# An encoder block in one launch: the low halves of 56 stationary factors on VectorE instead of in an adding DMA, and w_down's plain chunk at the other end

## The chip, the cores and the metric

The kernel runs on one core of one Trainium2 chip. The metric is the device time of one execution in microseconds, the median of several runs.

## The reference

One layer of a streaming encoder on 512 positions with 2048 channels, all float32. A mixer (a projection, two causal depthwise convolutions, a gate, a layer norm, an output projection) comes first and is not touched. Behind it stands the MLP, which is what the change is about:

```python
m = rms_norm(h, mlp_pre_gain[l])
z = jnp.square(jax.nn.relu(jnp.einsum("bsd,df->bsf", m, w_up[l])))      # 2048 -> 8192
z = jnp.einsum("bsf,fd->bsd", z, w_down[l])                             # 8192 -> 2048
h = h + rms_norm(z, mlp_post_gain[l])
```

## The kernel before, in words

**Float32 products from two halves.** TensorE multiplies rounded values (type fp32r). Every factor is therefore kept as a high half, which is the value rounded by a copy on ACT, and a low half, which is the value less its high half. A product is three matmuls: high by low, low by high, high by high.

**Seven products instead of eight.** Most of the work goes by Strassen's scheme with seven products for a 2 x 2 arrangement of blocks. `by_seven` (L367) does a pair of output tiles of w_up with seven calls of `product` (L360), 24 matmuls each, in the order r11, t2, t1, r21, t3, r22, t4. `wide_seven` (L945) does the same for w_down, on one chunk of z and two blocks of 512 output columns, in seven groups of 24 matmuls. Sums of blocks of the weights and of the activations are made on VectorE beforehand. The first eight tiles of w_up, and one of the eight chunks of w_down's product, are plain: no seven products and no sums.

**Where stationary factors come from.** `Stationary` (L109) is one long list of jobs, one for each 128 x 1024 factor of w_in, w_out, w_up and w_down in the order of use. A raw weight block is loaded by SyncE (`load`, L119) into one of six raw buffers. A job's value is a raw block or a sum of blocks (VectorE, L163 for w_up, L195 for w_down). `prepare` (L228) makes the high half on ACT (L237) two jobs ahead of the low half, and the low half on VectorE (L246). `take` (L252) asks for the factors of the next product and prepares three or four more. In w_up's pairs the seventh job, and in w_down's units the eleventh and twelfth (`22a`, `22b`), are raw blocks, and for these 28 + 28 jobs the low half is made in another way: ACT writes minus the high half (L240), and a DMA that adds, issued by GpSimd (POOL in the profile), brings the raw block from HBM a second time and adds it to that (L241).

**Buffers.** One pool of 43 slots of 128 x 1024 holds all halves, sums, z tiles and moving factors. During w_up about thirty of them hold the moving side for the whole stage; the rest turn over. A slot is written again when its last reader is done, which for a z tile's half is the DMA that stores it.

**z.** w_up's output tile pairs, each a z tile of 128 x 2 x 512, go through `keep_z` (L783): relu, square and the high half on ACT (L790, L791, L796), the low half on VectorE (L340, the line of the helper `add`), and both halves stored to z_dram by DMAs that ACT issues (L811). Chunk c is made of z tiles 4c to 4c + 3. A chunk that is used in seven products also needs the sums of its blocks: two more VectorE steps, a high and a low half, two more stores. These steps are a queue of small jobs, `z_jobs`: three jobs a tile without sums, six with them. Each product of w_up runs one job, or two when more than eight are queued (L891), and each group of `wide_seven` runs one.

**w_down.** Chunks 0 to 6 go through `wide_seven`, four blocks of 512 columns in two calls each, and are added up in SBUF; while a chunk's second call runs, the next chunk's factors are loaded from z_dram (`load_factor`, L896, on SyncE's queue between the weights). Chunk 7 is plain and comes last: half of it in `wide_tile` (L1004), the other half in the loop that ends the kernel, row block by row block, with the norm and the output behind each. PSUM has seven banks for products; in both seven-schemes a bank is reused by a later product that adds onto it, so VectorE's evacuation (L340) must have read it by then.

**Order.** Nothing is scheduled by a tool: each engine's instructions stand in the order in which this code issues them. Evacuations are put off by one product (`pending`, L341).

## Time and profile before

| | |
|---|---|
| median of 3 runs | 2028.47 us (2028.08 to 2035.81) |
| the profiled execution | 2024.5 us, span 2022.8 us |
| mean granted TensorE clock | 0.987 of full speed |
| TensorE busy | 1919.6 us (95%) |
| VectorE busy | 1563.1 us (77%) |
| ScalarE (ACT) busy | 914.3 us (45%) |
| GpSimd (POOL) busy | 129.6 us (6%) |
| DMA moved | 372.17 MB, mean 184 GB/s |

The mixer takes the first 640 us or so. The MLP's norm and its plain tiles follow, the products of seven of w_up run from about 722 to 1358 us, w_down's from 1358 to about 1915, and its plain chunk ends the kernel. In a row of the timeline the first number is the start, the second how long, and in brackets stands how long the engine was idle before it and what ended that. In a row of waits stand the sum, how often, and the longest.

### The profile page before, as it was taken

The page shows a single profiled execution, that of the slowest core. Times are in us where ns is not written, and L with a number is a line of the kernel's source. Part 1 is how long each engine was busy: PE and PEld are TensorE (multiplying, and loading weights), DVE is VectorE, ACT ScalarE, POOL GpSimd, SP SyncE. Part 2 cuts the span into 40 slices and gives each one's busy share as a digit, 9 for nine tenths or more (in the row PEclk, how much of TensorE's full clock was granted, in tenths as well). Part 3 has the DMA queues.
Part 4 walks back from the last instruction along what each step waited for, and adds up shares of the span by engine and source line. Part 5 has one row for each costly group of instructions (what it writes and reads, how often), then busy time and mean ns, then how long its engine had stood idle before and what let it go on. Part 6 is the DMA issues. An engine that isn't in the chain of part 4 may idle for free.

```text
span 2022.8 us, 28179 instructions
## 1 busy us (share of the span) xinstructions
PE 1919.6 (95%) x11050; PEld 1696.6 (84%) x11050; DVE 1563.1 (77%) x1932; ACT 914.3 (45%) x1114; POOL 129.6 (6%) x126
## 2 busy tenths in 40 slices
PE   8999999999999977899999999898999999999998
PEld 6888888888998867899999999887887877877876
DVE  8899898669767767777877877758678787787748
ACT  6222121444445455555565565546534343353343
POOL 4000011201110000000000000000000000000000
PEclk9999999999999988999999999999999999999999
DMA  7233323233367357777777777677875866768732
GB/s 250 87 104 104 104 84 104 83 117 92 111 201 257 98 167 229 219 218 218 211 211 227 214 214 226 200 251 227 269 229 167 280 199 219 260 189 256 266 110 84
DMA packets 154357, 372.17 MB, mean 184 GB/s; under 512 B 12144, under 2 KB 75760, under 8 KB 154224
## 3 DMA queue, kind: packets, MB, share of 16 engines
q1 hardware_dynamic: 78192, 270.04, 40.6%
q10 hardware_dynamic: 67968, 70.96, 10.2%
q0 software_dynamic: 8064, 29.36, 7.6%
q8 instruction: 87, 1.43, 0.3%
q14 instruction: 46, 0.38, 0.1%
HBM read 295.35 MB, written 74.97 MB: 183 GB/s over the span
## 4 chain that ended last, share of the span: by engine, by line
PE 29%; DMA 16%; DVE 8%; issue 6%; ACT 4%; SPq 0%; ACTq 0%; DVEq 0%; POOLq 0%
PE bank L935 24%; DMA z_dram<-slot 7%; DMA slot<-w_up_in 6%; PE bank L299 4%; DVE slot L246 2%; DMA raw<-w_down_in 2%; DVE slot L340 2%; ACT slot L237 2%; DVE slot L163 1%; DVE slot L195 1%; DMA raw<-w_up_in 1%; ACT slot L791 1%; ACT slot L790 1%; ACT slot L796 0%; DVE raw L163 0%
## 5 line engine op out<-in xcount | busy, mean ns | idle before, releaser
L299 PE MATMUL bank<-slot,slot 128*128 128x256 f32 (+1 forms) x7584 | 1143.9, 313 | 64.5 <-DMA slot<-w_up_in 33.6
L299 PEld LDWEIGHTS bank<-slot,slot 128*128 128x128 f32 x7584 | 1057.5, 192 | 150.3 <-DMA slot<-w_up_in 38.5
L935 PE MATMUL bank<-slot,slot 128*128 128x512 f32 x2736 | 631.3, 392 | 19.3 <-DVE slot L340 11.6
L935 PEld LDWEIGHTS bank<-slot,slot 128*128 128x128 f32 x2736 | 514.8, 189 | 132.2 <-DVE slot L340 13.7
L237 ACT ACTIVATE slot<-raw 128x1024 fp32r<-128x1024 f32 x336 | 345.7, 1050 | 244.7 <-DVE raw L163 108.0
L237 ACT ACTIVATE slot<-slot 128x1024 fp32r<-128x1024 f32 x208 | 218.9, 1057 | 382.9 <-DVE slot L195 211.1
L246 DVE TENSOR_TENSOR slot<-raw,slot 128x1024 fp32r<-128x1024 f32 x280 | 349.8, 1263 | 46.1 <-ACT slot L237 40.5
L246 DVE TENSOR_TENSOR slot<-slot,slot 128x1024 fp32r<-128x1024 f32 x208 | 254.1, 1222 | 60.4 <-PE bank L299 23.3
L340 DVE TENSOR_TENSOR slot<-slot,slot 128x1024 fp32r<-128x1024 f32 (+2 forms) x128 | 104.7, 824 | 102.2 <-DMA z_dram<-slot 47.9
L510 DVE SCALAR_TENSOR_TENSOR slot<-slot,par_sb,slot 128x512 f32<-128x512 f32 x240 | 162.9, 743 | 0.0
L340 DVE TENSOR_TENSOR slot<-slot,bank 128x512 f32<-128x512 f32 x208 | 133.9, 680 | 27.8 <-PE bank L935 27.8
L195 DVE TENSOR_TENSOR slot<-slot,raw 128x1024 f32<-128x1024 f32 x28 | 34.3, 1225 | 78.2 <-DMA raw<-w_down_in 77.7
L94 ACT ACTIVATE slot<-tmp 128x512 fp32r<-128x512 f32 (+1 forms) x40 | 21.9, 583 | 155.4 <-DVE tmp L543 117.5
L319 PE MATMUL bank<-slot,slot 128*128 128x512 f32 (+1 forms) x216 | 80.6, 373 | 6.2 <-ACT slot L94 6.2
L321 PE MATMUL bank<-slot,slot 128*128 128x512 f32 (+1 forms) x216 | 80.5, 373 | 2.9 <-DVE slot L98 2.9
L320 PE MATMUL bank<-slot,slot 128*128 128x512 f32 (+1 forms) x216 | 80.3, 372 | 1.5 <-DVE slot L246 1.5
L241 POOL DMA_DIRECT2D slot<-w_up_in x28 | 24.5, 875 | 717.2 <-DVE slot L340 399.5
L796 ACT ACTIVATE slot<-slot 128x1024 fp32r<-128x1024 f32 x60 | 63.4, 1056 | 12.7 <-DVE slot L340 9.7
L417 POOL TENSOR_TENSOR sum<-sum,tmp 128x512 f32<-128x512 f32 x35 | 59.4, 1698 | 94.5 <-ACT tmp L421 93.3
L240 ACT ACTIVATE slot<-slot 128x1024 fp32r<-128x1024 f32 x56 | 59.4, 1060 | 1.8
L241 POOL DMA_DIRECT2D slot<-w_down_in x28 | 24.4, 870 | 527.8 <-ACT slot L240 375.5
L319 PEld LDWEIGHTS bank<-slot,slot 128*128 128x128 f32 x216 | 41.4, 192 | 13.1 <-ACT slot L94 6.2
(101 smaller groups left out, 982.5 us busy)
## 6 DMA issues: line engine op xcount, KB each, us to landing
raw<-w_up_in SPq DMA_DIRECT2D x128, 512.0 KB, 4.5
z_dram<-slot ACTq DMA_DIRECT2D x120, 512.0 KB, 5.9
slot<-z_dram SPq DMA_DIRECT2D x106, 512.0 KB, 8.2
raw<-w_down_in SPq DMA_DIRECT2D x100, 512.0 KB, 4.5
raw<-w_in_in SPq DMA_DIRECT2D x76, 512.0 KB, 4.4
raw<-w_out_in SPq DMA_DIRECT2D x32, 512.0 KB, 4.1
slot<-w_up_in POOLq DMA_DIRECT2D x28, 512.0 KB, 8.6
slot<-w_down_in SPq DMA_DIRECT2D x28, 512.0 KB, 5.9
```

The costliest lines, as they stand in the source:

```text
L237: nc.scalar.activation(hi, value, AF.Copy)
L240: nc.scalar.activation(lo, hi.bitcast(F32), AF.Copy, scale=-1.0)
L246: nc.vector.tensor_tensor(lo, value, hi.bitcast(F32), op=ALU.subtract)
L299: nc.tensor.matmul(ps, s, m, start=n == 0 and not onto, stop=n == len(todo) - 1, skip_group_check=onto)
L319: nc.tensor.matmul(ps[:, cols], hi, mhi, start=first, stop=False)
L320: nc.tensor.matmul(ps[:, cols], lo, mhi, start=False, stop=False)
L321: nc.tensor.matmul(ps[:, cols], hi, mlo, start=False, stop=last)
L340: add = lambda out, a, b, op=ALU.add: nc.vector.tensor_tensor(out, a, b, op=op)
L417: nc.gpsimd.tensor_tensor(self.total, self.total, t, op=ALU.add)
L510: nc.vector.scalar_tensor_tensor(out=acc, in0=g[:, k : k + S], scalar=w, in1=acc, op0=ALU.mult, op1=ALU.add)
L796: nc.scalar.activation(made["hi", g].rearrange("p f w -> p (f w)"), value.rearrange("p a b -> p (a b)"), AF.Copy,)
L935: matmul = lambda a, b, first=False, last=False: nc.tensor.matmul(ps, a, b, start=first, stop=last, skip_group_check=onto)
```

## The change

It has two parts.

First, the adding DMA goes. Every job of `Stationary` has its low half made on VectorE (L246 before, L239 after). With it go 56 copies on ACT (L240), 56 DMAs on POOL's queue (L241) and the second reading of those blocks. The low half's slot is taken when VectorE's instruction is issued and no longer with the high half, and the raw block of such a job is read last by VectorE and no longer by ACT.

Second, the plain chunk is chunk 0 instead of chunk 7. `wide_seven` runs over chunks 1 to 7, and chunk 0 still comes last. The z tiles without sums are thus the first four, not the last four, and the last four have them. The host lays w_down out accordingly. The queue of z jobs is drained by two from more than six on.

```diff
-            self.jobs.append((lambda: self.get(n), n + 1, None))
+            self.jobs.append((lambda: self.get(n), n + 1))
...
-                (lambda: self.get(n22), 4, odd[1] if added_up else None),
+                (lambda: self.get(n22), 4),
...
-                (lambda: raw("22a"), 5, units["22a"]),
-                (lambda: raw("22b"), 6, units["22b"]),
+                (lambda: raw("22a"), 5),
+                (lambda: raw("22b"), 6),
...
-                    hi, lo = slot([P, WCOLS], F32R), None
+                    hi = slot([P, WCOLS], F32R)
                     nc.scalar.activation(hi, value, AF.Copy)
-                    if added is not None:
-                        lo = slot([P, WCOLS], F32R)
-                        nc.scalar.activation(lo, hi.bitcast(F32), AF.Copy, scale=-1.0)
-                        nc.gpsimd.dma_start(lo, added, accum_op=ALU.add)
-                    self.high.append((value, hi, lo))
-                value, hi, lo = self.high[len(self.parts)]
-                if lo is None:
-                    lo = slot([P, WCOLS], F32R)
-                    nc.vector.tensor_tensor(lo, value, hi.bitcast(F32), op=ALU.subtract)
+                    self.high.append((value, hi))
+                value, hi = self.high[len(self.parts)]
+                lo = slot([P, WCOLS], F32R)
+                nc.vector.tensor_tensor(lo, value, hi.bitcast(F32), op=ALU.subtract)
...
-        if c == N_CHUNK - 1:
+        if c == 0:
             z_jobs.append([lambda: store(0, 1)])
             return
...
-        z_job(2 if len(z_jobs) > 8 else 1)
+        z_job(2 if len(z_jobs) > 6 else 1)
...
-    for c in range(N_CHUNK - 1):
-        following = WIDE_ORDER if c < N_CHUNK - 2 else FACTORS[:4]
+    for c in range(1, N_CHUNK):
+        following = WIDE_ORDER if c + 1 < N_CHUNK else FACTORS[:4]
+        c_next = (c + 1) % N_CHUNK
...
-        wide_tile(t, N_CHUNK - 1, range(CHUNK // 2), last_step)
+        wide_tile(t, 0, range(CHUNK // 2), last_step)
...
-                    ps, plain_block(N_CHUNK - 1, k, b), b % 2, parts[t, i // 2], i % 2,
+                    ps, plain_block(0, k, b), b % 2, parts[t, i // 2], i % 2,
```

TensorE's and SyncE's instructions stand in the same order before and after; only VectorE's, ACT's and POOL's lists differ. Line numbers shift by seven: L340 before is L333 after, L246 is L239, L195 and L163 stay.

VectorE in a regular pair of w_up, from the low half of a z tile (`slot<-slot,slot`) on, through an evacuation (`tmp<-tmp,bank`) and the sums of that z tile (128x512 and twice 128x256) to the next pair's sums of weights. Before:

```order
L340 TENSOR_TENSOR slot_7737<-slot_7409,slot_7701 128x1024
L340 TENSOR_TENSOR tmp_7657<-tmp_7656,bank_7739 128x256
L340 TENSOR_TENSOR slot_7772<-slot_7409 128x512
L340 TENSOR_TENSOR slot_7772<-slot_7409,slot_7772 128x256 x2
L163 TENSOR_TENSOR slot_7800<-raw_7694,raw_7696 128x1024
L163 TENSOR_TENSOR slot_7801<-slot_7800,raw_7523 128x1024
```

And after:

```order
L333 TENSOR_TENSOR slot_6711<-slot_6387,slot_6678 128x1024
L239 TENSOR_TENSOR slot_6740<-raw_6429,slot_6705 128x1024
L333 TENSOR_TENSOR tmp_6634<-tmp_6633,bank_6713 128x256
L333 TENSOR_TENSOR slot_6748<-slot_6387 128x512
L333 TENSOR_TENSOR slot_6748<-slot_6387,slot_6748 128x256 x2
L163 TENSOR_TENSOR slot_6776<-raw_6671,raw_6673 128x1024
L163 TENSOR_TENSOR slot_6777<-slot_6776,raw_6500 128x1024
```

One instruction is new, the second: the low half of the pair's seventh factor.

VectorE in the first pair of seven, from the evacuation of the third product (`tmp<-tmp,bank`) to that of the fifth (`slot<-tmp,bank`); L95 is the low half of an activation sum. Before:

```order
L340 TENSOR_TENSOR tmp_5866<-tmp_5865,bank_5977 128x256
L95 TENSOR_TENSOR slot_5436<-slot_5756,slot_5436 128x256
L95 TENSOR_TENSOR slot_5486<-slot_5756,slot_5486 128x256
L340 TENSOR_TENSOR slot_6018<-slot_5531,slot_6015 128x1024
L163 TENSOR_TENSOR slot_6044<-raw_5920,raw_5922 128x1024
L163 TENSOR_TENSOR slot_6045<-slot_6044,raw_5701 128x1024
L246 TENSOR_TENSOR slot_6050<-raw_5701,slot_6002 128x1024
L340 TENSOR_TENSOR slot_6054<-slot_5531 128x512
L340 TENSOR_TENSOR slot_6054<-slot_5531,slot_6054 128x256 x2
L246 TENSOR_TENSOR slot_6087<-slot_6045,slot_6048 128x1024
L340 TENSOR_TENSOR slot_5863<-tmp_5866,bank_6060 128x256
```

And after:

```order
L333 TENSOR_TENSOR tmp_5866<-tmp_5865,bank_5972 128x256
L95 TENSOR_TENSOR slot_5436<-slot_5756,slot_5436 128x256
L95 TENSOR_TENSOR slot_5486<-slot_5756,slot_5486 128x256
L163 TENSOR_TENSOR slot_6038<-raw_5920,raw_5922 128x1024
L163 TENSOR_TENSOR slot_6039<-slot_6038,raw_5701 128x1024
L239 TENSOR_TENSOR slot_6044<-raw_5701,slot_5997 128x1024
L333 TENSOR_TENSOR slot_6048<-slot_5703,slot_6012 128x1024
L239 TENSOR_TENSOR slot_6077<-slot_6039,slot_6042 128x1024
L333 TENSOR_TENSOR slot_5863<-tmp_5866,bank_6050 128x256
```

The sums are gone, and the low half of a z tile (L333, 128x1024) that stands here is of the tile after the one before. Just ahead of this place one more pair of sums is gone and one low half of a factor is new.

VectorE in a unit of w_down, the evacuations of two groups (`slot<-slot,bank`), two instructions each. Before:

```order
L340 TENSOR_TENSOR slot_13094<-slot_13094,bank_13725 128x512
L340 TENSOR_TENSOR slot_13094<-slot_13094,bank_13726 128x512
L340 TENSOR_TENSOR slot_13097<-slot_13097,bank_13769 128x512
L340 TENSOR_TENSOR slot_13097<-slot_13097,bank_13770 128x512
L246 TENSOR_TENSOR slot_13842<-slot_13598,slot_13806 128x1024
```

And after:

```order
L333 TENSOR_TENSOR slot_13064<-slot_13064,bank_13691 128x512
L333 TENSOR_TENSOR slot_13064<-slot_13064,bank_13692 128x512
L239 TENSOR_TENSOR slot_13764<-raw_13415,slot_13726 128x1024
L239 TENSOR_TENSOR slot_13770<-raw_13488,slot_13762 128x1024
L333 TENSOR_TENSOR slot_13067<-slot_13067,bank_13732 128x512
L333 TENSOR_TENSOR slot_13067<-slot_13067,bank_13733 128x512
L239 TENSOR_TENSOR slot_13806<-slot_13564,slot_13768 128x1024
```

The low halves of `22a` and `22b` now stand between the two groups' evacuations.

More of the change, by code (lines that the diff above doesn't have):

```diff
@@ L172, in p7 @@
                 return sub(self.get(n11), self.get(n11), self.get(n21))
-            for value, frees, added in (
-                (lambda: self.get(n11), 0, None),
-                (p6, 0, None),
-                (lambda: s["1"], 0, None),
-                (lambda: self.get(n12), 0, None),
-                (p7, 2, None),
-                (lambda: sub(s["2"], self.get(n12), s["2"]), 0, None),
-                (lambda: self.get(n22), 4, odd[1] if added_up else None),
+            for value, frees in (
+                (lambda: self.get(n11), 0),
+                (p6, 0),
+                (lambda: s["1"], 0),
+                (lambda: self.get(n12), 0),
+                (p7, 2),
+                (lambda: sub(s["2"], self.get(n12), s["2"]), 0),
+                (lambda: self.get(n22), 4),
             ):
-                self.jobs.append((value, n11 + frees if frees else 0, added))
+                self.jobs.append((value, n11 + frees if frees else 0))
         def strassen_wide(self, units):
@@ L208, in s2 @@
                 return sub(s[u], s[u], raw("11" + u))
-            for value, frees, added in (
-                (lambda: s1("a"), 0, None),
-                (lambda: s1("b"), 0, None),
-                (lambda: s2("a"), 0, None),
-                (lambda: s2("b"), 0, None),
-                (lambda: raw("11a"), 0, None),
-                (lambda: raw("11b"), 0, None),
-                (lambda: sub(raw("11a"), raw("11a"), raw("21a")), 2, None),
-                (lambda: sub(raw("11b"), raw("11b"), raw("21b")), 4, None),
-                (lambda: sub(s["a"], last["a"], s["a"]), 0, None),
-                (lambda: sub(s["b"], last["b"], s["b"]), 0, None),
-                (lambda: raw("22a"), 5, units["22a"]),
-                (lambda: raw("22b"), 6, units["22b"]),
-                (lambda: last["a"], 0, None),
-                (lambda: last["b"], 0, None),
+            for value, frees in (
+                (lambda: s1("a"), 0),
+                (lambda: s1("b"), 0),
+                (lambda: s2("a"), 0),
+                (lambda: s2("b"), 0),
+                (lambda: raw("11a"), 0),
+                (lambda: raw("11b"), 0),
+                (lambda: sub(raw("11a"), raw("11a"), raw("21a")), 2),
+                (lambda: sub(raw("11b"), raw("11b"), raw("21b")), 4),
+                (lambda: sub(s["a"], last["a"], s["a"]), 0),
+                (lambda: sub(s["b"], last["b"], s["b"]), 0),
+                (lambda: raw("22a"), 5),
+                (lambda: raw("22b"), 6),
+                (lambda: last["a"], 0),
+                (lambda: last["b"], 0),
             ):
-                self.jobs.append((value, first + frees if frees else 0, added))
+                self.jobs.append((value, first + frees if frees else 0))
         def prepare(self, upto):
@@ L279, in encoder_block @@
     for m in range(UP_PLAIN, N_UP, 2):
-        W.strassen(w_up[m], w_up[m + 1], True)
+        W.strassen(w_up[m], w_up[m + 1])
     down_units = iter(range(w_down.shape[0]))
@@ L906, in load_first @@
         for name in WIDE_ORDER[3 * (n == 3) : 3 + (n == 3)]:
-            load_factor(0, name)
+            load_factor(1, name)
     for m in range(UP_PLAIN, N_UP, 2):
@@ L945, in wide_seven @@
     def wide_seven(c, t, after):
-        if c == 0:
+        if c == 1:
             for name in ((t, 0), (t, 1), (t + 1, 0), (t + 1, 1), None):
@@ L985, in wide_seven @@
                     )
-                evacuate(accumulate, c == 0 and first, sums[to][j], ps)
+                evacuate(accumulate, c == 1 and first, sums[to][j], ps)
             after(q)
@@ L1186, in _down_units @@
     units = []
-    for c in range(N_CHUNK - 1):
+    for c in range(1, N_CHUNK):
         for t in range(0, N_WIDE, 2):
@@ L1191, in _down_units @@
                 units.append(unit(c, odd + 4 * (name[2] == "b"), 2, t + int(name[0]) - 1))
-    c, half = N_CHUNK - 1, CHUNK // 2
+    c, half = 0, CHUNK // 2
     for at in (0, half):
```

13 lines of the change are left out of this document (6 added, 7 removed).

## The prediction

> **What bounds the kernel now.** I read the page first: the busy shares, the span in 40 slices and the DMA queues.
>
> ```profile
> span 2022.8 us, 28179 instructions
> PE 1919.6 (95%) x11050; PEld 1696.6 (84%) x11050; DVE 1563.1 (77%) x1932; ACT 914.3 (45%) x1114; POOL 129.6 (6%) x126
> ...
> PE   8999999999999977899999999898999999999998
> DVE  8899898669767767777877877758678787787748
> PEclk9999999999999988999999999999999999999999
> DMA  7233323233367357777777777677875866768732
> ...
> q0 software_dynamic: 8064, 29.36, 7.6%
> ...
> slot<-w_up_in POOLq DMA_DIRECT2D x28, 512.0 KB, 8.6
> ```
>
> TensorE is the bound, and what can be won is its idle time and its slow clock. Both are thickest where the up projection's products of seven begin (slices 15 and 16). From there on DMA is seven tenths busy, and part of that is the adding DMA: 0.5 MB each, 8.6 us from issue to landing. The waits of TensorE alone, and then busy time by stage (the up stage's beginning, its regular part, and the products of w_down; columns PE, PEld, DVE, ACT, POOL, granted clock, DMA), say what it waits for.
>
> ```profile
> PE bank L299 <- DMA slot<-w_up_in: 33.6, 24, 2.6
> PE bank L299 <- ACT slot L237: 15.1, 2, 10.0
> PE bank L299 <- DVE slot L340: 13.8, 2, 12.5
> PE bank L935 <- DVE slot L340: 11.6, 5, 2.9
> ```
>
> ```profile
> 720.00:862.00 142.00, 110.49 (x861) 109.34 (x860) 104.56 (x127) 80.89 (x93) 4.50 (x5) 0.89 0.73 219
> 862.00:1340.00 478.00, 447.05 (x3669) 442.59 (x3668) 373.54 (x430) 275.15 (x304) 19.13 (x22) 1.00 0.73 213
> 1400.00:1880.00 480.00, 468.37 (x2053) 385.86 (x2052) 376.33 (x399) 204.89 (x208) 20.91 (x24) 1.00 0.71 224
> ```
>
> TensorE's timeline shows each wait in its place.
>
> ```profile
> 745.28 22.49 PE L299 MATMUL bank<-slot,slot 128*128 128x256 f32 x168 [12.45 <-DVE slot L340]
> 777.74 21.76 PE L299 MATMUL bank<-slot,slot 128*128 128x256 f32 x169 [9.97 <-ACT slot L237]
> 825.57 23.10 PE L299 MATMUL bank<-slot,slot 128*128 128x256 f32 x168 [5.09 <-ACT slot L237]
> 849.97 20.51 PE L299 MATMUL bank<-slot,slot 128*128 128x256 f32 x169 [1.30 <-DVE slot L340]
> ...
> 1157.19 20.42 PE L299 MATMUL bank<-slot,slot 128*128 128x256 f32 x168 [1.39 <-DMA slot<-w_up_in]
> 1179.28 20.41 PE L299 MATMUL bank<-slot,slot 128*128 128x256 f32 x168 [1.67 <-DMA slot<-w_up_in]
> ...
> 1382.50 17.89 PE L935 MATMUL bank<-slot,slot 128*128 128x512 f32 x66 [4.92 <-ACT slot L925]
> ...
> 1620.38 76.58 PE L935 MATMUL bank<-slot,slot 128*128 128x512 f32 x336 [1.66 <-DVE slot L340]
> ```
>
> A pair of up tiles is 168 matmuls and takes 20.4 us of TensorE. In the regular part 22 pairs take 478 us, 21.7 each, and the 1.3 us between is the wait for the adding DMA ahead of the pair's last product. VectorE is busy 373.5 / 22 = 17.0 us a pair. So TensorE waits there for one transfer while VectorE has 4.7 us to spare.
>
> **The adding DMAs, up stage.** One pair of the regular part, its engines together:
>
> ```profile
> 1189.62 1.23 DVE L340 TENSOR_TENSOR slot<-slot,slot 128x1024 fp32r<-128x1024 f32 x1 [1.04 <-ACT slot L796]
> 1190.57 1.06 ACT L240 ACTIVATE slot<-slot 128x1024 fp32r<-128x1024 f32 x1
> 1190.97 0.42 DVE L340 TENSOR_TENSOR tmp<-tmp,bank 128x256 f32<-128x256 f32 x1
> 1192.04 0.86 POOL L241 DMA_DIRECT2D slot<-w_up_in  x1 [20.74 <-DVE slot L340]
> ...
> 1200.51 14.65 PE L299 MATMUL bank<-slot,slot 128*128 128x256 f32 x120 [0.82 <-DMA slot<-w_up_in]
> 1200.52 1.23 DVE L340 TENSOR_TENSOR slot<-slot,slot 128x1024 fp32r<-128x1024 f32 x1 [2.16 <-DMA z_dram<-slot]
> 1201.66 1.22 DVE L246 TENSOR_TENSOR slot<-slot,slot 128x1024 fp32r<-128x1024 f32 x1
> ...
> 1211.53 1.23 DVE L340 TENSOR_TENSOR slot<-slot,slot 128x1024 fp32r<-128x1024 f32 x1 [1.72 <-ACT slot L796]
> ```
>
> Now the low half of the pair's seventh factor is begun by L240 at 1190.57, issued by POOL at 1192.04 and complete some 8.5 us later, when TensorE starts the product, at 1200.51. After the change VectorE makes it directly behind its row at 1189.62: done near 1192, seven microseconds and more ahead of its use. The wait goes: at most 33.6 us. In its place stands one more L246 on VectorE, 1.15 us from start to start (1200.52 to 1201.66), 28 times. It lies in the 2.16 us that VectorE waits in this pair, and 17.0 + 1.15 = 18.1 us fit under TensorE's 20.4. Without that cover it would come back whole, 28 x 1.15 = 32 us. SyncE loses a little: a raw buffer comes free behind L246 instead of behind ACT's copy, about a microsecond later. POOL's queue holds nothing else here.
>
> What is late next is VectorE's row at 1200.52. It writes the low half of a z tile's sums into the buffer of the row at 1189.62, whose store to z_dram must have landed. The group of such rows in the regular part (22 pairs) holds most of VectorE's waiting:
>
> ```profile
> L340 DVE TENSOR_TENSOR slot<-slot,slot 128x1024 fp32r<-128x1024 f32 x41 | 50.2, 1225 | 79.1 <-DMA z_dram<-slot 40.2 <-ACT slot L796 29.5 <-ACT slot L237 9.4
> ```
>
> On ACT's queue that store stands behind L240, so it is issued 1.06 us earlier without it. VectorE's loop, now 10.9 + 11.0 us, becomes 10.9 - 1.06 = 9.8 to the row at 1200.52 (its own work there is 8.4 + 1.15 = 9.5) and 11.0 - 1.72 = 9.3 from there, if the wait for ACT goes because VectorE comes later: 19.1 us, below TensorE's 20.4. I leave 3.6 us of the waits standing: **-30 us** (bounds -14 with a loop of 21.1 us, which is a rival below, and -33.6).
>
> **Early z tiles without sums.** Each of the first four z tiles loses its sums (1.5 us of VectorE), their low half (1.2 us), their copy on ACT (1.06 us), two stores and three buffers. All of that now stands between 724 and 850, where the stalls of 12.45, 9.97, 5.09 and 1.30 us lie, 28.8 together. The first: TensorE stops at 732.8 until VectorE's evacuation of the fifth product.
>
> ```profile
> 724.89 0.69 DVE L340 TENSOR_TENSOR slot<-slot 128x512 f32<-128x512 f32 x1
> ```
>
> From this row to that evacuation VectorE now needs 20.2 us: seven wide rows of 1.15 (counted in the orders shown with the change), two sums of 1.5, seven narrow rows of 0.4 make 13.9, and 6 us are waits for ACT, which has this tile's and the next one's work too. After: eight wide rows and seven narrow ones, 12 us, with some 2 of waiting since ACT's list there is no shorter (one copy and L240 gone, two squarings come earlier). The evacuation comes near 739 and 6 to 7 us of the stall stay. The next two stalls are the backlog of the four tiles' sums, which is gone: I leave 2 us of 16.4. Sum **-20 us** (bounds -8, the first stall's share alone, and -28.8).
>
> **The clock.** After these three stalls, the same 168 matmuls took 22.49, 21.76 and 23.10 us against 20.42 and 20.41 after waits of 1.39 and 1.67: 6.1 us lost, of which the first stall keeps about one. **-5 us**. [...]
>
> **The products of w_down.** The sums of the last four z tiles come here or just ahead; VectorE has the room, for it waits 14 us for a load as the stage begins. An L240 is gone from ACT ahead of the 4.92 us wait at 1382.50: **-1 us** (+5 if the late sums, 1.5 + 1.2 us on VectorE and 1.06 on ACT a tile, delay it instead). In the regular part:
>
> ```profile
> 1363.51 1.23 DVE L195 TENSOR_TENSOR slot<-slot,raw 128x1024 f32<-128x1024 f32 x1 [14.01 <-DMA raw<-w_down_in]
> ...
> 1579.61 0.86 POOL L241 DMA_DIRECT2D slot<-w_down_in  x1 [1.17 <-DMA slot<-z_dram]
> ...
> 1591.95 0.42 SPq L122 DMA_DIRECT2D raw<-w_down_in  x1
> ...
> 1600.89 1.23 DVE L195 TENSOR_TENSOR slot<-slot,raw 128x1024 f32<-128x1024 f32 x1 [8.22 <-DMA raw<-w_down_in]
> ...
> 1619.65 2.47 DVE L340 TENSOR_TENSOR slot<-slot,bank 128x512 f32<-128x512 f32 x4
> ```
>
> Once per chunk VectorE waits some 8 us for a load that SyncE could issue only behind the factor loads, which wait for TensorE; then it works without a gap until 1619.65, and TensorE waits 1.66 us for the first of those four. No adding DMA is in flight between 1591.95 and 1600.89 (the unit's last is issued at 1579.61 and needs some 8.5), so the load lands no earlier. The two new L246 stand behind the second of the four additions, so the wait at 1620.38 stays as it is, and the third and fourth come 2.3 us later, near 1623, before TensorE needs their bank, one group of 24 matmuls (5.5 us) after 1620.38. 376.3 + 24 x 1.15 = 404 of 480 us: VectorE holds. **0 us** (bounds -11.6, all five waits gone, and +16, half of 28 x 1.15 on the path).
>
> **Sum.** -30 - 20 - 5 - 1 + 0 = -56 us. The profiled execution took 2024.5 us (span 2022.8 and 1.7 around it), so 1968.5; the median of the runs shown is 2028.5, 4 us above it, so I forecast **1972.5 us**. A change of 0.5%, 10 us, is about the least that a measurement of this kernel can tell from none.
>
> **Rivals.** (A) The buffers decide: the wait behind the z_dram store stays and VectorE's loop is 21.1 us. The store lands as late as now (10.9) and half of the wait for ACT stays (9.3 + 0.9). For it: 40.2 us of that wait in 22 pairs, and a z tile's second low half takes the buffer of the first after the change too. Against: the store leaves earlier and shares the DMA engines with less. The regular part then gives 28 x 0.6 = 17, the beginning 13 with its clock: about 1999. (B) w_down also gains: less DMA brings its loads forward, the 11.6 us of waits go and the first stall goes wholly: 1972.5 - 12 - 8 = 1953. For it: software DMA held 7.6% of 16 engines' span. Against: no adding transfer overlaps the late load. (C) Slower: VectorE's waits are one fixed chain with ACT, and each added L246 lengthens it. Place: every pair and every pair of w_down units; price 28 x 1.15 = 32 and 28 x 1.15 = 32, less the beginning's 20: about 2072. It decides from the point where VectorE's 4.7 us of idle time per pair don't shrink by 1.15. [...] (D) No change to tell: pairs stay at 21.7 us, the beginning gives its 25 and w_down takes its bound of 16: 2020.
>
> **How the numbers follow.** Forecast 0.58 (its own range 1960 to 1988), A 0.20, B 0.12, C 0.05, D 0.05. The range leaves out C and D and what lies past the ends of A and B by more than a few microseconds: 1950 to 2006. Faster: forecast, A and B, 0.90; same: D, 0.05; slower: C, 0.05.
>
> **What would show it.** Right: no TensorE wait for slot<-w_up_in, pairs at 20.4 to 20.6 us with VectorE near 18.1, one stall of 6 to 7 us after the first product of seven and none over 3 after it, w_down waits still 2 us per chunk. Wrong: TensorE waiting for VectorE's L340 or ACT's L237 in every pair (A or C), a pair of 21 us or more, or w_down stalls that grow by over 1 us each.

## The result and the profile after

The changed kernel took 1946.76 us (median of 4 runs, 1945.55 to 1949.1), the kernel before 2028.28 us on the same chip: a ratio of 0.9591, 95% interval 0.9566 to 0.9616. That is 81.5 us less. The forecast was 1972.5 us with a range of 1950 to 2006: the direction was right and so was the mechanism in w_up; the time lies 25.7 us below the forecast and 3 us below the range, and w_down gained where nothing was forecast.

Lines moved: what was L340, L299, L935, L246, L237, L796 is L333, L292, L928, L239, L235, L789 in the changed kernel. First its page: shares, two rows of the 40 slices, and the landing time of the z stores.

```profile
span 1947.4 us, 27944 instructions
...
PE 1908.7 (98%) x11050; PEld 1690.3 (87%) x11050; DVE 1623.2 (83%) x1988; ACT 851.8 (44%) x1058; POOL 81.0 (4%) x70
...
PE   8999999999999998999999999989999999999998
...
DMA  7233323222347627666676666787564764755722
...
z_dram<-slot ACTq DMA_DIRECT2D x120, 512.0 KB, 3.4
```

TensorE is busy in 98% of the span, and the low slices 15 and 16 of before are gone. The same 11050 matmuls took 10.9 us less (1919.6 to 1908.7), which goes with the mean granted clock (0.987 before, 0.993 after); TensorE's idle time fell from 103.2 to 38.7 us. What is left of its longer waits in the two stages with seven products:

```profile
PE bank L292 <- ACT slot L235: 5.5, 1, 5.5
PE bank L928 <- DMA slot<-z_dram: 4.7, 1, 4.7
...
PE bank L928 <- DVE slot L333: 2.8, 3, 1.2
PE bank L928 <- ACT slot L918: 2.3, 1, 2.3
```

The 33.6 us behind the adding transfer are gone, and those behind VectorE's evacuations in w_down fell from 11.6 to 2.8. TensorE's timeline shows the stages:

```profile
725.99 10.33 PE L292 MATMUL bank<-slot,slot 128*128 128x256 f32 x72 [2.01 <-ACT tmp L341]
741.80 549.29 PE L292 MATMUL bank<-slot,slot 128*128 128x256 f32 x4536 [5.48 <-ACT slot L235]
...
1294.93 5.63 PE L928 MATMUL bank<-slot,slot 128*128 128x512 f32 x24
...
1474.61 152.69 PE L928 MATMUL bank<-slot,slot 128*128 128x512 f32 x672 [1.24 <-DVE slot L333]
...
1847.24 1.03 PE L1053 MATMUL bank<-tmp,slot 128*128 128x128 f32 x8
```

The second row is 4536 matmuls, as many as 27 pairs, without one gap: 20.34 us a pair against 21.7. The rows of regular stretches (PE, PEld, DVE, ACT, POOL, clock, DMA):

```profile
840.00:1292.00 452.00, 451.11 (x3738) 449.35 (x3737) 408.86 (x469) 257.07 (x290) 1.10 (x2) 1.00 0.68 210
1330.00:1805.00 475.00, 472.17 (x2079) 389.55 (x2078) 412.18 (x433) 183.50 (x188) 0.00 (x0) 1.00 0.59 203
```

VectorE works 408.86 / (452 / 20.34) = 18.4 us a pair, 90% of the stretch, and no longer waits for a z store; its waits for ACT's copy of a z tile (39.4 us in all) stay and do not reach TensorE in these pairs.

The stages of all kernels below are taken in the same way from TensorE's timeline: w_up from the first 128x256 product to the first 128x512 one, w_down from there to the first 128x128 one. Before, these rows start at 723.93, 1358.38 and 1922.42. So w_up's sevens went from 634.4 to 568.9 us (-65.5), w_down's from 564.0 to 552.3 (-11.7); what is ahead of them and behind them moved by +2.1 and -0.2.

### The profile page after: what moved, and what is told of

It reads as the page before. It is cut to its first block, busy times and chain, and to the rows that moved or that the text cites. A ratio compares the mean times of both kernels' runs of the same rounds, so it can differ in the third digit from the quotient of the medians.

```text
span 1947.4 us, 27944 instructions
## 1 busy us (share of the span) xinstructions
PE 1908.7 (98%) x11050; PEld 1690.3 (87%) x11050; DVE 1623.2 (83%) x1988; ACT 851.8 (44%) x1058; POOL 81.0 (4%) x70
## 3 DMA queue, kind: packets, MB, share of 16 engines
q10 hardware_dynamic: 67968, 70.96, 10.8%
## 4 chain that ended last, share of the span: by engine, by line
PE 90%; DVE 5%; ACT 2%; DMA 2%; issue 1%; SPq 0%; ACTq 0%; DVEq 0%
PE bank L292 56%; PE bank L928 28%; PE bank L314 2%; PE bank L313 2%; DVE slot L239 2%; PE bank L312 2%; DVE slot L333 1%; DMA raw<-w_down_in 1%; DVE slot L195 1%; ACT slot L235 1%; DMA tmp<-x_in 0%; DMA slot<-z_dram 0%; ACT slot L94 0%; PE bank L1053 0%; DVE slot L98 0%
## 5 line engine op out<-in xcount | busy, mean ns | idle before, releaser
L292 PE MATMUL bank<-slot,slot 128*128 128x256 f32 (+1 forms) x7584 | 1134.5, 312 | 8.4 <-ACT slot L235 5.5
L292 PEld LDWEIGHTS bank<-slot,slot 128*128 128x128 f32 x7584 | 1051.7, 191 | 90.7 <-ACT slot L235 6.7
L928 PE MATMUL bank<-slot,slot 128*128 128x512 f32 x2736 | 628.1, 391 | 10.5 <-DMA slot<-z_dram 4.7
L928 PEld LDWEIGHTS bank<-slot,slot 128*128 128x128 f32 x2736 | 513.4, 188 | 121.7 <-DVE slot L239 5.1
L239 DVE TENSOR_TENSOR slot<-raw,slot 128x1024 fp32r<-128x1024 f32 x336 | 417.4, 1257 | 49.5 <-ACT slot L235 40.3
L235 ACT ACTIVATE slot<-raw 128x1024 fp32r<-128x1024 f32 x336 | 342.4, 1050 | 194.9 <-DVE raw L163 66.7
L235 ACT ACTIVATE slot<-slot 128x1024 fp32r<-128x1024 f32 x208 | 219.4, 1058 | 450.8 <-DVE slot L195 199.1
L239 DVE TENSOR_TENSOR slot<-slot,slot 128x1024 fp32r<-128x1024 f32 x208 | 254.1, 1222 | 29.1 <-PE bank L292 19.2
L333 DVE TENSOR_TENSOR slot<-slot,bank 128x512 f32<-128x512 f32 x208 | 134.3, 681 | 14.1 <-PE bank L928 14.1
L333 DVE TENSOR_TENSOR slot<-slot,slot 128x1024 fp32r<-128x1024 f32 (+2 forms) x128 | 104.6, 823 | 41.3 <-ACT slot L789 39.4
L195 DVE TENSOR_TENSOR slot<-slot,raw 128x1024 f32<-128x1024 f32 x28 | 34.3, 1225 | 57.2 <-DMA raw<-w_down_in 56.6
L789 ACT ACTIVATE slot<-slot 128x1024 fp32r<-128x1024 f32 x60 | 63.4, 1056 | 1.0
L312 PEld LDWEIGHTS bank<-slot,slot 128*128 128x128 f32 x216 | 41.8, 194 | 13.2 <-ACT slot L94 6.2
L314 PEld LDWEIGHTS bank<-slot,slot 128*128 128x128 f32 x216 | 41.8, 193 | 10.9 <-DVE slot L98 4.1
L313 PEld LDWEIGHTS bank<-slot,slot 128*128 128x128 f32 x216 | 41.7, 193 | 9.8 <-DVE slot L239 2.3
L333 DVE TENSOR_TENSOR tmp<-tmp,bank 128x256 f32<-128x256 f32 x76 | 31.7, 417 | 17.9 <-PE bank L292 17.9
```

Source lines behind the costliest of these rows:

```text
L195: nc.vector.tensor_tensor(out, a, b, op=op)
L235: nc.scalar.activation(hi, value, AF.Copy)
L239: nc.vector.tensor_tensor(lo, value, hi.bitcast(F32), op=ALU.subtract)
L292: nc.tensor.matmul(ps, s, m, start=n == 0 and not onto, stop=n == len(todo) - 1, skip_group_check=onto)
L312: nc.tensor.matmul(ps[:, cols], hi, mhi, start=first, stop=False)
L313: nc.tensor.matmul(ps[:, cols], lo, mhi, start=False, stop=False)
```

## The experiments

One table ahead, in us; "before" and "after" are the two kernels, waits are TensorE's for the 0.5 MB transfers of POOL's queue. Times are medians; stages and waits are of the one profiled execution of each kernel.

```
                                       time     w_up  w_down  waits
before                                 2028.3   634.4  564.0   33.6
after                                  1946.8   568.9  552.3    -
no adding, chunk as before             1960.6   583.3  550.5    -
chunk moved, adding kept               2022.8   625.3  567.9   37.4
after, adding back in w_down           1962.6   568.9  569.1    -
after, adding back in w_up             2003.8   630.6  549.0   40.0
before, plain loads in place of adding 1998.9   617.8  551.7   23.5
before, adding begun one job earlier   2038.2   637.7  566.2    0
after, ACT's copies written over       1976.8   592.8  557.2    -
after, copies unread                   1951.4   572.0  552.1    -
  and plain loads unread               2019.0   641.0  555.7    -
  and adding transfers unread          2061.5   666.3  564.8    -
after, copies unread and held          1962.4   580.6  555.3    -
  and plain loads                      1973.4   588.4  558.3    -
  and adding transfers                 2002.4   591.1  584.7    -
```

**The two halves of the change.** The first kernel is the one before without adding transfers (two edits):

```
-                (lambda: raw("22a"), 5, units["22a"]),
-                (lambda: raw("22b"), 6, units["22b"]),
+                (lambda: raw("22a"), 5, None),
+                (lambda: raw("22b"), 6, None),
...
-        W.strassen(w_up[m], w_up[m + 1], True)
+        W.strassen(w_up[m], w_up[m + 1])
```

> The kernel before with one half of the change: no adding DMA anywhere, the low halves of the seventh factors made by VectorE; the plain chunk is still the last, so the first four z tiles still make sums. Theory (the adding DMA is behind two terms, the pairs' wait in w_up of 33.6 us and the w_down gain of 11.7 us, and the z tiles' sums behind the stalls at the beginning): no TensorE wait for slot<-w_up_in, w_down stage near 552 us, beginning with most of its 28.8 us of stalls: about 2028.3 - 33.6 - 11 = 1984, between 1975 and 1992. Rival (the w_down gain comes from the chunk's move, not from the adding DMA): w_down stage near 563 us, about 1995. Rival A of the prediction (the buffers decide once the transfer is gone): the regular part at 21.1 us a pair, above 2000.

The second is the one before with the chunk's half of the diff, the adding transfers kept:

```
-        if c == N_CHUNK - 1:
+        if c == 0:
...
-        z_job(2 if len(z_jobs) > 8 else 1)
+        z_job(2 if len(z_jobs) > 6 else 1)
...
-    for c in range(N_CHUNK - 1):
+    for c in range(1, N_CHUNK):
```

> The kernel before with the other half of the change: the first chunk of w_down's product is the plain one, the first four z tiles make no sums; the adding DMAs of w_up and w_down stay. Theory: the 28.8 us of stalls at the beginning shrink to about 5 to 7, the pairs keep their wait for the adding DMA (33.6 us), the w_down stage stays near 564 us: about 2028.3 - 23 - 5 of the clock = 2000, between 1993 and 2010. Rival (the w_down gain belongs to the chunk's move): w_down near 553 us and about 1989. If the two halves add up, this gain and that of the first half alone sum to the whole of 81.5 us; if each opens room for the other, to less.

The first took 1960.64 us, 0.9643 (0.9621 to 0.9666) of before, the second 2022.75 us, 0.9953 (0.9929 to 0.9977); before was 2031.74 here. The gains, 71.1 and 9.0 us, add up to 80.1, about the whole. The adding transfers are nearly nine tenths of it. Both expectations missed their ranges. The first had 44 us: in w_up it lacked 10.8 us of stalls and 6.9 of slower matmuls (TensorE's busy time there fell from 572.0 to 565.1). The second had 28, which the chunk's move does not bring by itself. TensorE at the beginning, without adding (first fence) and with the chunk moved (second):

```profile
746.22 22.52 PE L299 MATMUL bank<-slot,slot 128*128 128x256 f32 x168 [9.91 <-DVE slot L340]
775.80 62.96 PE L299 MATMUL bank<-slot,slot 128*128 128x256 f32 x504 [7.05 <-ACT slot L237]
```

```profile
742.34 21.84 PE L299 MATMUL bank<-slot,slot 128*128 128x256 f32 x169 [8.00 <-ACT slot L237]
...
789.13 42.44 PE L299 MATMUL bank<-slot,slot 128*128 128x256 f32 x337 [2.87 <-DVE slot L340]
```

The four stalls of 28.8 us fall to 18.0 (with one of 1.05) by the first half alone and to 10.9 by the second alone; with both, 5.5 are left. So the stalls were not the sums' doing alone. With the transfers still there, what the second half wins at the beginning is partly spent again: TensorE's waits for them grow from 33.6 to 37.4 us, and w_up is only 9 us shorter. The w_down gain belongs wholly to the first half: 550.5 us without adding, 567.9 with the chunk moved alone, which is 3.9 us more than before.

**One stage at a time.** Now the changed kernel, with the adding transfers and ACT's second copy back in one stage alone; the edits are the two of the first kernel, one each.

> The changed kernel, with the adding DMAs (and ACT's second copy) put back in w_down alone. Theory (the adding DMAs slow the loads and the evacuation in w_down): the w_down stage back near 563 us, the load that VectorE waits for once a chunk back from 7.0 to about 8.9 us: about 1946.8 + 11 = 1958. Rival (the w_down gain comes from the chunk's move or from the up stage): no change, 1946 to 1949. The prediction's own step said that no adding DMA overlaps the late load, by which this is no change too.

> The changed kernel, with the adding DMAs (and ACT's second copy) put back in w_up alone. Theory (the pairs' wait is the adding transfer's own landing): TensorE waits for slot<-w_up_in again in 22 to 27 pairs, pairs near 21.7 us, w_down unchanged near 552 us: about 1946.8 + 34 = 1981, between 1975 and 1990. Rival (the wait was only the late start behind z tiles' sums and a busy ACT, so that with the early sums gone the transfer begins in time): some 10 us, about 1957.

With adding in w_down: 1962.55 us, w_up unchanged to 0.1 us, w_down 569.1. With adding in w_up: 2003.81 us, w_down 549.0, w_up 61.7 longer. Each stage carries its own cost, and both cost more than was expected (1958, and 1975 to 1990). Of the 61.7 us in w_up, 47.2 are idle time of TensorE, 40.0 of that in its waits for the transfer itself, and 14.5 are slower matmuls (577.0 us busy against 562.6; granted clock of the whole execution 0.989 against 0.993). That w_down is 5 us slower here than before (569.1 and 564.0) is not explained; the kernel with the chunk moved alone shows the same.

The wait in w_down of the kernel with adding there, and its late load:

```profile
PE bank L935 <- DVE slot L340: 13.0, 5, 3.2
```

```profile
1528.71 0.42 SPq L122 DMA_DIRECT2D raw<-w_down_in  x1
...
1538.82 1.23 DVE L195 TENSOR_TENSOR slot<-slot,raw 128x1024 f32<-128x1024 f32 x1 [9.38 <-DMA raw<-w_down_in]
```

The same load in the changed kernel:

```profile
1524.31 0.42 SPq L122 DMA_DIRECT2D raw<-w_down_in  x1
...
1531.34 1.23 DVE L195 TENSOR_TENSOR slot<-slot,raw 128x1024 f32<-128x1024 f32 x1 [6.31 <-DMA raw<-w_down_in]
```

From issue to use it takes 10.1 us with adding transfers and 7.0 without; before it was 8.9. In all three it is issued at the same place, 0.55 us behind the start of an evacuation of VectorE, and from that use to VectorE's evacuation at the chunk's end stand 18.8 us of unbroken work. So what the load loses, the evacuation loses, and TensorE what goes beyond its slack. The windows around the load show how full the DMA engines are, before and after (last two columns: DMA share, GB/s). Before, the two adding transfers were issued at 1577.57 and 1579.61, and the trace has them land 10.0 and 11.8 us later, at 1587.6 and 1591.4:

```profile
1574.00:1581.00 7.00, 7.00 (x33) 5.79 (x32) 4.50 (x6) 6.80 (x7) 1.73 (x2) 1.00 0.90 294
1581.00:1588.00 7.00, 7.00 (x33) 5.79 (x32) 6.26 (x8) 1.35 (x2) 0.00 (x0) 1.00 1.05 280
1588.00:1595.00 7.00, 7.00 (x33) 5.79 (x32) 4.64 (x5) 2.12 (x2) 0.00 (x0) 1.00 1.03 370
1595.00:1602.00 7.00, 7.00 (x32) 5.81 (x31) 1.11 (x1) 0.00 (x0) 0.00 (x0) 1.00 1.03 413
```

```profile
1507.00:1514.00 7.00, 7.00 (x33) 5.79 (x32) 6.94 (x9) 4.61 (x5) 0.00 (x0) 1.00 1.00 325
1514.00:1521.00 7.00, 7.00 (x32) 5.79 (x31) 6.26 (x7) 1.66 (x2) 0.00 (x0) 1.00 0.94 354
1521.00:1528.00 7.00, 7.00 (x32) 5.82 (x31) 4.00 (x5) 1.52 (x2) 0.00 (x0) 1.00 0.86 293
1528.00:1535.00 7.00, 7.00 (x32) 5.80 (x31) 3.62 (x4) 2.35 (x3) 0.00 (x0) 1.00 0.97 362
```

Before, the share reads 1.03 to 1.05 from 1581 to 1602, so the engines are full, and they move only 280 GB/s in the first seven of these microseconds, while both adding transfers are under way. Other loads fall behind: a weight load that SyncE issued at 1586.12 lands at 1595.7, 3.8 us after the late load was issued. After, the same weight load (issued at 1518.47) lands 0.5 us behind the late load's issue, and the share falls to 0.86 at 1521 to 1528. This way from the adding to the late load is read from these rows. That adding costs w_down its time does not rest on it: the next kernel shows that.

**Bytes or adding.** The kernel before, whose transfers load the same bytes into the same buffers and wait for the same things, without adding:

```
-                        nc.gpsimd.dma_start(lo, added, accum_op=ALU.add)
+                        nc.gpsimd.dma_start(lo, added)
```

> The kernel before, whose 56 transfers on POOL's queue are plain loads of the same bytes into the same buffers, with no adding (so the seventh products' low halves are wrong, and ACT's second copy is overwritten). Everything waits for what it waited for. Theory (the adding itself is dear: 29.36 MB took 7.6% of 16 engines' span, 191 GB/s, against 270.04 MB in 40.6%, 329 GB/s, on the queue of the plain loads): landing falls from 8.6 us to 5 to 6, the wait for slot<-w_up_in falls from 33.6 us to under 5, w_down stays within 4 us of 564: about 1990, between 1980 and 2000. Rival (the bytes and the queue cost it, not the adding): landing near 8 us, waits as before, 2020 to 2030. If the w_down stage falls to 552 too, it was the adding that held up the late load, not the half megabyte.

It took 1998.94 us, 0.9831 (0.9811 to 0.985). Its page and waits:

```profile
q0 software_dynamic: 8064, 29.36, 4.6%
...
slot<-w_up_in POOLq DMA_DIRECT2D x28, 512.0 KB, 7.9
```

```profile
PE bank L299 <- DMA slot<-w_up_in: 23.5, 22, 2.7
```

The same 29.36 MB cost 4.6% of 1993.3 us, 92 us of 16 engines, in place of 7.6% of 2022.8, 154 us: 1.68 times as much for adding. w_down falls to 551.7 us with the bytes still moving, and nothing but the adding differs, so it was the adding that cost it. The transfers' own landing in w_down falls from 8.5 to 7.1 us, and the late load, issued at 1570.10 here, takes 7.6 us from issue to use, where it was 8.9. In w_up the landing falls only from 8.6 to 7.9 us and 23.5 us of the waits stay. Of the 51.1 us that w_up loses against the kernel without transfers (634.4 and 583.3), 34.5 stay with plain ones: there most of the cost is that TensorE waits for a transfer at all. The time lies in the expected range by luck: that the landing would come down to 5 or 6 us and the waits to under 5 was wrong, and the 12.3 us of w_down, where at most 4 were expected, made up for it. The runs show the factor, 1.68, and not its reason.

**Is the wait all, in w_up?** If the transfer starts one job earlier, its landing should no longer matter:

```
-                while len(self.high) < min(len(self.parts) + 2, len(self.jobs)):
+                while len(self.high) < min(len(self.parts) + 3, len(self.jobs)):
```

> The kernel before with its adding DMAs, where ACT makes each factor's high half, and so begins the adding transfer, one job earlier (3 ahead instead of 2). Theory (in w_up the loss is only the transfer's landing time against its start, 1.3 us a pair short): the waits for slot<-w_up_in go, 33.6 to under 5 us, the w_down stage stays near 564 us or above: about 1995, between 1985 and 2005. Rival (the DMA engines and VectorE behind the z_dram stores set the pace while adding transfers run): pairs stay above 21 us, 2010 or above.

This kernel takes some low halves of w_down from values that are already written over; the work is the same. It took 2038.22 us, 1.0027 (1.0014 to 1.0039). Waits of TensorE, then of VectorE:

```profile
PE bank L299 <- DVE slot L340: 56.1, 26, 11.6
```

```profile
DVE slot L246 <- DMA z_dram<-slot: 39.5, 22, 4.0
```

TensorE waits for the transfer not once, and from 870 to 1306 us the pairs still take 21.2 to 24 us: VectorE now waits for a z store to give a buffer free, and TensorE for VectorE. The rival held: taking away the wait for the transfer alone wins nothing here. But one more buffer is in use in this kernel, and TensorE begins the products of seven 9.4 us later than before, so it does not tell how much of the second chain is the transfers' and how much the buffer's and the other order's.

Next the transfers without anyone waiting. First ACT's copies back in the changed kernel, into the early buffer of before, which VectorE then writes over:

```
+                    if added is not None:
+                        lo = slot([P, WCOLS], F32R)
+                        nc.scalar.activation(lo, hi.bitcast(F32), AF.Copy, scale=-1.0)
```

> The changed kernel, with ACT's second copy of each seventh factor (56 of 1.06 us) and its early buffer put back, but no adding DMA: VectorE overwrites the buffer. Theory (the transfers alone cost the time; ACT's copies and the longer-held buffers lie beside other work): 1946 to 1950, no wait of TensorE for ACT grows by over 3 us in all. Rival (the copies on ACT, ahead of the z_dram stores and of the first factors, made part of the loss): up stage 5 us or more longer, 1952 or above.

It took 1976.81 us, 0.9719 (0.9703 to 0.9735): 30 us more than the changed kernel (26 by the two ratios), against the theory. VectorE's and TensorE's rows say why (line numbers here are one less than before's):

```profile
1201.65 1.23 DVE L245 TENSOR_TENSOR slot<-raw,slot 128x1024 fp32r<-128x1024 f32 x1 [0.81 <-ACT slot L240]
```

```profile
PE bank L298 <- DVE slot L339: 21.0, 27, 0.9
```

The experiment had put in a wait of its own: VectorE writes the buffer that ACT's copy writes, waits 0.81 us for it in each pair, and TensorE waits 0.7 to 0.8 us in each. VectorE has 2 us a pair to spare on average, and none at that place. With the copies in a buffer that nobody reads:

```
+                        spare = slot([P, WCOLS], F32R)
+                        nc.scalar.activation(spare, hi.bitcast(F32), AF.Copy, scale=-1.0)
```

> The changed kernel with ACT's second copy of each seventh factor (56 of 1.06 us) put back into a buffer of the same pool that nobody reads; VectorE makes the low half in a buffer of its own and waits for no such copy. Nothing of the result is left out. Theory (ACT's copies are hidden; what the kernel with the copies written over by VectorE lost was its 0.8 us wait for the copy in each pair): 1945 to 1951, pairs at 20.34 us. Rival (ACT's time itself, or one buffer less, delays VectorE): pairs above 20.8 us, 1960 or more.

It took 1951.41 us, with 19 pairs in a row without a gap and three waits of 0.8 to 0.9 us: ACT's copies themselves are nearly free (3 us in w_up). Onto that buffer a plain load, and in a third kernel an adding one:

> As the last one, and then POOL's queue loads half a megabyte into that unread buffer, plainly (56 transfers, the bytes of the kernel before). Theory (plain bytes on POOL's queue are nearly free when nobody waits for them): w_down stage 550 to 555 us, up stage within 6 us of the changed kernel's 569, no wait of VectorE for z_dram stores that reaches TensorE: 1946 to 1956. Rival (the traffic alone holds up the z_dram stores, whose landing is 6.0 us with such loads against 3.4 without, and by them VectorE and TensorE): pairs above 20.8 us, 1962 or more.

> As the last one, but the 56 transfers add, as in the kernel before; still nobody reads what they make. Theory (in w_up TensorE's wait for the transfer was the cost, in w_down the DMA engines' time for adding, which brings the late load later): up stage within 8 us of 569, w_down 562 to 570: 1957 to 1970. Rival (the adding traffic alone also slows w_up, through the z_dram stores): pairs at 21 us or more, up stage 585 or more, 1975 or more.

They took 2018.97 and 2061.5 us, the second slower than before (1.0163, 1.0144 to 1.0182). In w_down the numbers are about those of the theory: 552.1, 555.7 and 564.8 us for copies, plain and adding. In w_up they failed as experiments. Three rows of the plain one:

```profile
970.66 4.61 PE L299 MATMUL bank<-slot,slot 128*128 128x256 f32 x20 [3.73 <-DVE slot L340]
...
970.10 0.42 DVE L340 TENSOR_TENSOR slot<-tmp,bank 128x256 f32<-128x256 f32 x1 [1.21 <-DMA slot<-w_up_in]
...
970.03 0.38 ACT L348 ACTIVATE slot<-bank 128x256 f32<-128x256 f32 x1 [2.76 <-DMA slot<-w_up_in]
```

The pool gave the unread buffer to the next z tile, and ACT and VectorE waited for the transfer's landing in TensorE's place. In w_down too VectorE's rows at L195 and L246 waited for it, 17.1 us in all with plain transfers and 40.4 with adding ones, so those two numbers are not clean either. So three more kernels follow, in which a read of one element a row on VectorE holds the buffer for four jobs (two in w_down):

```
+                if self.held and self.held[0][0] <= len(self.parts):
+                    nc.vector.tensor_copy(warm, self.held.popleft()[1].bitcast(F32)[:, :1])
```

> The changed kernel with ACT's second copies into an unread buffer, which is now held for four more jobs in w_up and two in w_down by a read of one element a row on VectorE (56 small instructions). No transfers: the control of the next two. Theory (copies and one or two more buffers in use cost little): 1948 to 1958, pairs under 20.6 us. Rival (a buffer held for 12 us more starves the z tiles): 1965 or more.

> As the control, with a plain load of half a megabyte on POOL's queue into each held buffer. Theory (bytes nobody waits for cost w_up nearly nothing): within 8 us of the control, pairs under 20.8 us, w_down within 5 us of the control's. Rival (traffic slows the z_dram stores and raw loads until VectorE is late in every pair): 20 us or more above the control.

> As the last one, but the transfers add. Theory (w_up lost only TensorE's wait; w_down loses the adding's time on the DMA engines): up stage within 8 us of the control's, w_down 9 to 16 us longer: 10 to 25 us above the control. Rival (the adding also slows w_up by itself): up stage 20 us or more longer, 30 us or more above the control in all.

They took 1962.43, 1973.4 and 2002.39 us, all three more than expected. The control itself is 8.6 us slower in w_up than without the hold (580.6 and 572.0), and the other two are 11.0 and 40.0 us above it. In w_up, 580.6, 588.4 and 591.1: transfers that nobody waits for cost 8 us plain and 11 us adding, where those that TensorE waits for cost 61.7. TensorE's waits for VectorE in w_up, in the three kernels (VectorE's evacuations at L340 are L344 and L345 here):

```profile
PE bank L303 <- DVE slot L344: 7.5, 23, 1.1
```

```profile
PE bank L304 <- DVE slot L345: 15.4, 22, 3.9
```

```profile
PE bank L304 <- DVE slot L345: 16.7, 24, 3.0
```

So w_up lost mostly by the waits, and the traffic alone is about a sixth of the loss. In w_down the last two fail as measurements:

```profile
DVE warm L246 <- DMA slot<-w_down_in: 46.8, 24, 4.7
```

```profile
DVE warm L246 <- DMA slot<-w_down_in: 79.5, 28, 6.8
```

There the read itself waits for the landing, 46.8 us of VectorE with plain transfers and 79.5 with adding ones. For w_down the kernel with plain loads in place of adding (551.7 us against 564.0) and the one with adding in w_down alone (569.1) stand.

**Further on from the changed kernel.** Its last stall in w_up, 5.48 us, waits for ACT by the trace. One kernel puts the z tiles' work off by two products, the other takes one ACT pass off each of the first four z tiles:

```
+        if next(early) > 1:
+            z_job(2 if len(z_jobs) > 6 else 1)
```

> The changed kernel, in which the first two products of seven issue no work on the z tiles, so that ACT makes the first weight factors earlier (it copies the second product's factor at 740.63, behind four z tiles' squarings of 3.2 us each). Theory (the one stall left at the beginning, 5.48 us, is ACT's backlog): the stall falls by 3 us or more, 1940 to 1944. Rival (the stall only moves to a later product, or z buffers held longer cost as much): 1945 to 1949.

```
-            nc.scalar.activation(zt, zt, AF.Relu)
+            if c:
+                nc.scalar.activation(zt, zt, AF.Relu)
...
-            nc.scalar.activation(zt[:, i, :], ps, AF.Copy)
+            nc.scalar.activation(zt[:, i, :], ps, AF.Relu)
```

> The changed kernel, whose first four z tiles are cut at zero as ACT takes them out of PSUM, so that ACT has one pass of 1.06 us less for each of them where TensorE's stall of 5.48 us waits for ACT. The result is the same. Theory (that stall is ACT's backlog, and work taken away shortens it where work put off only moved it): the stall falls to about 2 us, 1942 to 1945. Rival (the stall goes over to VectorE, as when the work was put off): 1946 to 1950.

The first took 1949.17 us, 0.9587 (0.9573 to 0.9601) of before: the stall became one of 4.5 and one of 3.7 us, as the rival had it. The second took 1944.92 us, 0.9587 (0.9573 to 0.9601), not to be told from the changed kernel's 0.9591. That its time lies in the expected range shows nothing, for the stall kept its size:

```profile
737.71 549.60 PE L292 MATMUL bank<-slot,slot 128*128 128x256 f32 x4536 [5.77 <-ACT slot L235]
```

Its size hides what happened. Counted from the first product of seven, the stall ends after 14.7 us in place of 15.8, 1.1 us earlier, about the one pass that ACT is spared. But the three products ahead of it took 8.9 us, as in the kernel before at a granted clock of 1.00, in place of 10.3 at 0.84 in the changed kernel, so TensorE stood still earlier too. The two rows that end the stall in the changed kernel:

```profile
740.63 1.06 ACT L235 ACTIVATE slot<-raw 128x1024 fp32r<-128x1024 f32 x1 [0.36 <-issue]
741.24 0.41 DVE L333 TENSOR_TENSOR slot<-tmp,bank 128x256 f32<-128x256 f32 x1
```

ACT's copy ends at 741.69 and VectorE's evacuation at 741.65; TensorE starts at 741.80. In the kernel with one pass less they end at 737.60 and 737.56. So VectorE comes out at the same time as ACT, though only ACT is named, and in the changed kernel it works from 735.38 to there without a gap. Which of the two sets the stall stays open; no kernel took work off VectorE there.

## Why the prediction was wrong, and where it was right

The step that failed is the term of 0 us for w_down's regular part. By the prediction's own terms, against the profiled executions (span -75.4 us where -56 were forecast):

- **Adding transfers in w_up**, forecast -30: the waits are gone whole, -33.6, which was the bound. VectorE's loop, of which I feared that it would keep 3.6 us, keeps up with TensorE's 20.34 us a pair, and its work of 18.4 us is near the 18.1 of the text. (In the pair shown there, VectorE's own work up to the row at 1200.52 was 8.15 us and not 8.4; nothing hangs on it.) The kernels with held buffers show the cause: mostly the wait, and little of the traffic.
- **Early z tiles**, forecast -20: -23.3, from 28.8 to 5.48 us. One long stall is left, after the third product of seven, of 5.5 us where 6 to 7 were expected. That is partly luck: the three products ahead of it took 10.33 us, at a granted clock of 0.84, in place of 8.89 at 1.00 before; with those 8.89 it would have been 6.9, an estimate from these two rows. And the reason was half right: without the sums alone 10.9 us are left, without the transfers alone 18.0; it took both.
- **Clock**, forecast -5: -10.9 by TensorE's busy time for the same matmuls (-9.4 in w_up, -2.9 in w_down, +1.4 elsewhere). The text counted the three long stalls of w_up, 6.1 us. In w_down the granted clock of before was 0.72 in the 10 us behind the wait of 4.92 us at 1382.50, and 0.83 behind that of 2.87 us at 1540.62, where 336 matmuls took 78.11 us against 76.45 behind the wait of 2.13 us at 1778.16, with a clock of 1.00; in the pairs it was 0.92 behind one short wait (last section).
- **w_down's start**, forecast -1: two waits of 7.0 us in all, where the two rows of before hold 6.8. Nothing came of it.
- **w_down's regular part**, forecast 0: -8.8 (11.6 to 2.8 us), and 1.7 us of slower matmuls behind the longest of its waits (under Clock). This is the step that failed: "No adding DMA is in flight between 1591.95 and 1600.89 (the unit's last is issued at 1579.61 and needs some 8.5), so the load lands no earlier". The first half is true, by half a microsecond: the last transfer needed 11.8 us and landed at 1591.4. The conclusion is false. When that transfer had landed, the weight load issued at 1586.12 had not: it came in at 1595.7, 9.6 us after its issue, against 6.3 for the same load after the change, and the late load landed 8.8 us after its issue, against 6.9 after the change. With plain loads of the same bytes TensorE's five waits were 0.3 to 0.4 us each, against 1.7 to 2.9. Rival B named the outcome ("less DMA brings its loads forward") and I gave it 0.12. The argument against it looked at what overlaps the load and not at how long the engines had been full ahead of it. That transfers of GpSimd's queue hold up a load of SyncE's stands on one run: with adding transfers, and ACT's second copy, back in w_down alone, the load's use moved from 7.0 to 10.1 us after its issue.
- **From the profiled time to the median**, +4: before, the profiled execution lay 4 us under the median; after, it lies 2.3 over it. That 6.3 us difference is not explained by anything here.

The misses of the terms are 3.6, 3.3, 5.9, -1.2 and 8.8 us, together 20.4, against the 19.4 by which the span missed. With the last point's 6.3 that makes the 25.7 us between 1972.5 and 1946.8. With w_down's waits as forecast, the time would have been near 1956, inside the range. But the 5.9 us of the clock, or the 6.3 that nothing explains, would have been enough as well: the range was missed by several terms that were all too small, of which w_down's is the largest, and the one whose reason was wrong.

Rival C, VectorE as a fixed chain with ACT, did not come with the change. The kernel with the written-over buffer shows how near it was: there one wait of 0.8 us for ACT in each pair goes through to TensorE nearly whole.

## What to carry to other kernels

Ask of a DMA not only what overlaps the load that matters, but how long the engines have been full ahead of it; in this kernel the last adding transfer landed at 1591.4, and the load issued at 1591.95 still took 8.8 us, against 6.9 in the changed kernel. Where a busy engine takes over work that a transfer did, the price is read at the place in the pair where it stands, not from the share of busy time: here VectorE had 2 us a pair to spare, and its wait of 0.81 us reached TensorE as 0.7 to 0.8 us. And an experiment with an unread transfer needs a buffer that is held until the transfer has landed, or it measures the next owner's wait (here 2.76 us of ACT and 1.21 of VectorE in one place). A stall's size alone does not tell what a change did to it: read also where it begins and ends.

## What the hardware showed that was not expected

The adding transfers took 1.68 times the DMA engines' time of plain ones with the same bytes on the same queue (154 and 92 us for 29.36 MB), yet landed only 0.7 us later in w_up (8.6 and 7.9 us). And behind one short wait the granted clock was lower, behind another it was not. Two pairs of the kernel before, after waits of about 2 us:

```profile
916.16 21.91 PE L299 MATMUL bank<-slot,slot 128*128 128x256 f32 x168 [1.94 <-DMA slot<-w_up_in]
...
1048.40 20.41 PE L299 MATMUL bank<-slot,slot 128*128 128x256 f32 x168 [2.10 <-DMA slot<-w_up_in]
```

The first took 1.5 us longer for the same 168 matmuls, at a granted clock of 0.92; the second, after a longer wait, did not, at 1.00. The prediction's sum has nothing for the short waits, which holds for the two rows shown there and not for the first of these.
